# Linear attention's heads in staggered turns with finer steps, its gates' silu moved, weights cast further ahead in three jobs, and loads on GpSimd's queue

## The chip, the cores and the metric

The kernel runs on one core of a Trainium2 chip. A core has five engines with instruction streams of their own: TensorE (PE, with its weight loads as PEld), VectorE (DVE), ScalarE (ACT), GpSimd (POOL) and SyncE (SP). Each runs its stream in order; streams wait for each other by semaphores. Transfers between the device's memory and the core are issued by an engine onto its queue: SP and POOL do that here. The metric is the device time of one execution in microseconds, as the median of several runs.

## The reference

One layer of an encoder with 512 tokens and a width of 2048, in float32. The projection of the normalised input feeds two groups of heads, whose outputs are joined and projected; a gated feed-forward layer follows.

```python
h = rmsnorm(x) ; P = h @ W_in
# group A: 16 heads x 64, three dilated windows, merged
# group B: 4 heads of gated linear attention (dk 128, dv 256), both directions
G    = cumsum(log_a, within a chunk)
q_in = q * exp(G) ; k_in = k * exp(-G)
A    = (q_in @ k_in.T) * tril          # inside the chunk
S_t  = diag(a_t) S_{t-1} + k_t^T v_t   # across chunks
out_B = rmsnorm_per_head(o_fwd + o_bwd) * silu(gate)
x = x + concat(out_A, out_B) @ W_out
x = x + swiglu(rmsnorm(x)) ; rmsnorm at the end
```

What the change touches is group B: the four linear-attention heads (called heads 0 to 3 below), their output gates, and the weights of the projections beside which they run.

## The kernel before

**Jobs.** The large products are jobs, run one after the other by `run_job`: after the front part gqk0 and gv0 (queries, keys and values of the first two heads), gqk1 and gv1 (of the other two), gr0 and gr1 (the output gates, each four banks of results), then four jobs of the output projection, wo0 to wo3, then the feed-forward part. A job has 16 weight halves; for each half PE runs four banks of three matmuls (high by high, high by low, low by high part of the split numbers), 12 of 128x512. Kind A of job (gqk, gr) stands on lines L336 to L338, kind B (gv, wo) on L345 to L347.

**Weights.** `Stream` loads pieces of 512 KB on SP's queue (L209) into a few buffers and splits every half in two: ScalarE casts the high part (L237), VectorE subtracts it from the original (L218, the low part). At half i the split runs up to half i + AHEAD - 1 with AHEAD = 3. In the jobs called fine (gqk0 to gr1) the subtraction lags: it is issued at the next half's beginning. The load of a further piece waits in SP's stream until a buffer is free.

**Side work.** Beside the halves, `run_side` takes one step of the first `urgent` generator and one step of the `side` generator each time the credit reaches one; in a fine job the credit grows by a quarter of the job's rate after each bank (`RATES`, 2.5 for gqk and gv, 2.75 for gr), in wo by 1.0 after each half. The side generators are the low-rank forget gates, then the dilated attention (lines L536 to L700), then linear attention's heads.

**A head** (`gla`): softplus of the forget gates (L909 to L912), per direction a subtraction (L925), a scan along the tokens (L930), the chunk ends (L938 to L942), the centred sums (L945), exponentials (L943, L949, L950), the factors times queries and keys (L920), two products of PE with masks (L971, L977, L982, L991), the states between chunks (L1006 to L1025), the output products (L1053), a normalisation (L1061 to L1069), transposes (L1075) and a scaling (L1078). The heads run in pairs: `two(gla(0), gla(1))` takes one step of each in turn, started by the evacuation of gv0, and `two(gla(2), gla(3))` by that of gv1. A head's queries and keys, and a pair's values, are stored to memory by POOL (L825, L852) and come back by `load_gla` on SP's queue (L838, L842).

**The gates.** `evac_gr` multiplies the four banks by the normalisation's factors (L863) into four tiles of 128x512, applies silu at once (L868), and, for each head that is done, multiplies the head's output by it (L877) and splits the product into high and low part for the output projection (L408, L409).

Of the kernel before, what the change touches and what calls it, by code (L numbers as in the profile page):

```python
# [15 lines left out]
F32 = mybir.dt.float32  # L16
# [102 lines left out]
def layer(nc, tc, x, attn_norm_w, w_in, rel_table, gw_f, gb_f, gw_b, gb_b, gla_norm_w, w_out,  # L119
# [7 lines left out]
    with tc.manual_schedule(), \  # L127
# [48 lines left out]
        EXP_LN, SILU = "natural_log_exp_and_others", "silu_and_others"  # L176
        state = {"credit": 0.0, "set": None, "ahead": 0.0, "big": 0}

# [109 lines left out]
        class Job:  # L288
            fine = False
            drop = None  # L290
            between = None
# [15 lines left out]
        def run_job(j):  # L307
# [392 lines left out]
        def attention():  # L700
# [6 lines left out]
            for u in range(UNITS + 6):  # L707
                h = u // 4
                if u < UNITS:
                    if u % 8 == 2:  # L710
                        read_qk(h // 2 + 1)
                    if u % 8 == 5 and h // 2 + 1 < NH // 2:
                        urgent.append(load_qk(h // 2 + 1))
                    while h // 2 not in ready:
                        run_urgent()
                if "mix" in at:
                    pr = at.pop("mix")
                    mixh[pr] = split_of(mixf.pop(pr), big=pr > 4)
# [12 lines left out]
                if u % 2 == 0:  # L731
                    run(att_mix, (u - 6) // 2, UNITS // 2)
                run(att_norm, u - 1)
                if 33 <= u < 36:
                    load_v(1, ((0,), (1,), (2, 3))[u - 33])
                if u == UNITS - 3:
                    load_gla(0)
                    load_gla(1)
# [12 lines left out]

# [7 lines left out]
        gq, gk, gv = {}, {}, {}  # L759
        gate = {}  # L760
        gout = {}
# [66 lines left out]

        gla_there = []
        loaded = set()  # L830

        def load_gla(h):
            if h in loaded or h // 2 not in gla_there:
                return
            loaded.add(h)
            for d, i in ((gq, 0), (gk, 2)):
                d[h] = s2.get()
                sp.dma_start(out=d[h].t, in_=gqd[h // 2 * 4 + i + h % 2])  # L838
            if h % 2 == 0:
                gv[h // 2] = [s4.get(F32, [P, 2, 512]) for _ in range(2)]  # L840
                for i in range(2):
                    sp.dma_start(out=gv[h // 2][i].t.rearrange("p b c -> p (b c)"), in_=gvd[h + i])  # L842

        def evac_gv(pr):
            def f(banks):
                for t in range(4):
# [4 lines left out]
                    if t % 2:  # L851
                        pool.dma_start(out=gvd[2 * pr + t // 2], in_=v.t.rearrange("p b c -> p (b c)"))  # L852
                        put(v)
                gla_there.append(pr)
                side.append(two(gla(2 * pr), gla(2 * pr + 1)))
            return f

        def evac_gr(pr):
            def f(banks):
                ts = []  # L860
                for i in range(4):
                    t = s2.get()
                    dve.tensor_tensor(t.t, banks[i].t, rb[1].t, op=OP.mult)  # L863
                    put(banks[i])
                    ts.append(t)
                tables(SILU)
                for i in range(4):
                    act.activation(ts[i].t, ts[i].t, AF.Silu)  # L868
# [3 lines left out]
            return f  # L872

        def gla_out(i):
            if i in gate and i in gout:
                t, o = gate.pop(i), gout.pop(i)
                dve.tensor_tensor(o.t, o.t, t.t, op=OP.mult)  # L877
                put(t)
                mixf[8 + i] = o
                if not hT:  # L880
                    mixh[8 + i] = split_of(mixf.pop(8 + i), big=True)

# [6 lines left out]
        def gla(h):  # L889
# [14 lines left out]
            las = []  # L904
            tables(EXP_LN)
            for d in range(2):
                bcol = wcol[:, (B_F, B_B)[d] + h:(B_F, B_B)[d] + h + 1]
                l, m = s2.get(), s2.get()
# [6 lines left out]
                yield  # L915
            fs, qs, ks = [], [], []

# [3 lines left out]

            for d in range(2):
                c = fb[d]
                m, l = las[d]
                dve.tensor_tensor(m.t, m.t, l.t, op=OP.subtract)  # L925
                put(l)
                if d:
                    times(0)
                g = s2.get()
                dve.tensor_tensor_scan(g.t[:, c], G["res"][d].t[:, c], m.t[:, c], 0.0,  # L930
                                       op0=OP.mult, op1=OP.add)
                put(m)
                mid, end = ((63, 127), (64, 0))[d]
                f = sc[d]

                g3 = r3(g)
                if d == 0:
                    dve.tensor_tensor(f[:, 0:3], g3[:, 0:3, end], g3[:, 0:3, mid], op=OP.subtract)  # L938
                    dve.tensor_tensor(f[:, 0:3], f[:, 0:3], g3[:, 1:4, mid], op=OP.add)
                else:  # L940
                    dve.tensor_tensor(f[:, 0:3], g3[:, 1:4, end], g3[:, 1:4, mid], op=OP.subtract)
                    dve.tensor_tensor(f[:, 0:3], f[:, 0:3], g3[:, 0:3, mid], op=OP.add)  # L942
                act.activation(f[:, 0:3], f[:, 0:3], AF.Exp, scale=1.0 / TAU)  # L943
                gm = s2.get()
                dve.tensor_tensor(r3(gm), g3, g3[:, :, mid:mid + 1].to_broadcast([P, 4, P]), op=OP.subtract)  # L945
                put(g)
                yield
                q, k = s2.get(), s2.get()
                act.activation(q.t, gm.t, AF.Exp, scale=1.0 / TAU)  # L949
                act.activation(k.t, gm.t, AF.Exp, scale=-1.0 / TAU)  # L950
                put(gm)
                fs.append(f)
                qs.append(q)
                ks.append(k)
                yield
            times(1)
            yield
            put(gq.pop(h), gk.pop(h))
# [3 lines left out]
            T, kt = [], []  # L962
            as_, trs, ts = [], [], []
            for d in range(2):
                ts.append(s2.get())
                pool.memset(ts[d].t, 0.0)
            for d in range(2):
                a = ps.get()
                for b in range(4):
                    c = slice(b * P, (b + 1) * P)  # L970
                    mm(a.t[:, c], ks[d].t[:, c], qs[d].t[:, c], start=True, stop=True)  # L971
                as_.append(a)
            for d in range(2):
                tr = ps.get()
                for b in range(4):
                    c = slice(b * P, (b + 1) * P)
                    pe.transpose(tr.t[:, c], ks[d].t[:, c], idn)  # L977
                put(ks[d])
                trs.append(tr)
            for d in range(2):  # L980
                a, tr, t = as_[d], trs[d], ts[d]
                dve.copy_predicated(r3(t), masks[:, d:d + 1, :].to_broadcast([P, 4, P]),  # L982
                                    a.t.rearrange("p (b c) -> p b c", c=P))
                put(a)
                T.append(t)
                kk = s2.get()
# [5 lines left out]
            put(T[1])  # L992
            yield
            if h == 1:
                load_gla(2)
                load_gla(3)

# [68 lines left out]
            for i in range(2):  # L1066
                for b in (2 * i, 2 * i + 1):
                    c = slice((b % 2) * 256, (b % 2 + 1) * 256)
                    act.activation(on.t[:, b], os_[i].t[:, c], AF.Copy, scale=rs[:, b:b + 1])  # L1069
            put(*os_)  # L1070
            yield
            for i in range(2):
# [7 lines left out]
                gout[2 * h + i] = o  # L1080
            for i in range(2):
                gla_out(2 * h + i)
            yield
# [98 lines left out]
        n_front = len(jobs)  # L1182
        RATES = (2.5, 2.75)
        for pr in range(2):
# [11 lines left out]
        for j in jobs[n_front:]:  # L1196
            j.fine = True

        x1 = {}
# [914 lines left out]
```

## Time and profile before

| what | us |
|---|---|
| median of three runs | 2212.36 |
| lowest and highest run | 2211.18, 2214.01 |
| the profiled execution, its own time | 2214.81 |
| its span in the profile | 2213.0 |
| start of gr0's first matmul in it | 551.38 |

The profile has a page (busy time by engine, the span in slices, queues, the chain that ended last, the costliest groups) and views of the trace behind it: lists of waits, rows of one engine in order of time, and windows with each engine's busy time. A row in order of time reads: start, duration, engine, line, operation, output <- input, shape, and in brackets the idle time before it with what ended it. Rows of equal instructions in a run are folded (x8). Names in the profile are those of buffer classes: `a` holds tiles of 128x512, `b` tiles of 128x1024 or a pair of halves, `ps` the banks of results, `gqd` and `gvd` the stored queries, keys and values.

### The profile page before, as it was taken

The page shows a single profiled execution, that of the slowest core. Times are in us where ns is not written, and L with a number is a line of the kernel's source. Part 1 is how long each engine was busy: PE and PEld are TensorE (multiplying, and loading weights), DVE is VectorE, ACT ScalarE, POOL GpSimd, SP SyncE. Part 2 cuts the span into 40 slices and gives each one's busy share as a digit, 9 for nine tenths or more (in the row PEclk, how much of TensorE's full clock was granted, in tenths as well). Part 3 has the DMA queues.
Part 4 walks back from the last instruction along what each step waited for, and adds up shares of the span by engine and source line. Part 5 has one row for each costly group of instructions (what it writes and reads, how often), then busy time and mean ns, then how long its engine had stood idle before and what let it go on. Part 6 is the DMA issues. An engine that isn't in the chain of part 4 may idle for free.

```text
span 2213.0 us, 34591 instructions
## 1 busy us (share of the span) xinstructions
PE 2170.9 (98%) x12618; PEld 1908.3 (86%) x12618; DVE 1771.1 (80%) x3072; ACT 1200.8 (54%) x2197; POOL 333.1 (15%) x462
## 2 busy tenths in 40 slices
PE   9999999999889999999999999999999999999998
PEld 7888778888768888988888888888888899999987
DVE  5698757775575675898899989899899888988885
ACT  7454456776455243555555555555555565565562
POOL 0011221110000120011221111221121220011300
PEclk9999999999989999999999999999999999999999
DMA  5377774544225884367776767776777876576982
GB/s 189 123 189 173 186 222 130 177 140 130 90 66 170 287 298 149 100 167 188 174 194 176 183 179 184 187 183 185 177 183 183 254 186 200 177 187 155 280 312 76
DMA packets 257368, 397.81 MB, mean 180 GB/s; under 512 B 18925, under 2 KB 154269, under 8 KB 257198
## 3 DMA queue, kind: packets, MB, share of 16 engines
q1 hardware_dynamic: 203134, 276.69, 39.3%
q0 software_dynamic: 53744, 118.39, 24.1%
q8 instruction: 99, 1.62, 0.3%
q14 instruction: 71, 0.58, 0.1%
q10 hardware_dynamic: 320, 0.53, 0.1%
HBM read 285.37 MB, written 64.29 MB: 158 GB/s over the span
## 4 chain that ended last, share of the span: by engine, by line
PE 82%; issue 6%; DMA 5%; DVE 4%; ACT 2%; POOL 0%; DVEq 0%; ACTq 0%; SPq 0%; POOLq 0%
PE ps L1465 25%; PE ps L1451 13%; PE ps L346 6%; PE ps L345 6%; PE ps L347 6%; PE ps L1815 5%; PE ps L1816 5%; PE ps L1814 5%; DMA b<-a 4%; PE ps L338 2%; PE ps L336 2%; PE ps L337 2%; PE ps L650 1%; PE ps L1053 1%; DVE b L1374 1%
## 5 line engine op out<-in xcount | busy, mean ns | idle before, releaser
L1369 ACT CAST b<-b 128x768 fp32r<-128x768 f32 (+1 forms) x537 | 488.8, 945 | 349.9 <-DVE b L1374 162.3
L1374 DVE TENSOR_TENSOR b<-b,b 128x768 fp32r<-128x768 f32 (+1 forms) x537 | 563.8, 1084 | 35.1 <-ACT b L1369 24.2
L1465 PE MATMUL ps<-b,b 128*128 128x512 f32 x1552 | 451.0, 393 | 0.4 <-ACT b L1369 0.2
L1465 PE MATMUL ps<-a,b 128*128 128x512 f32 x1248 | 365.7, 394 | 4.2 <-DVE b L1485 4.2
L1465 PEld LDWEIGHTS ps<-b,b 128*128 128x128 f32 x1552 | 263.5, 188 | 30.7 <-ACT b L1369 0.7
L1451 PEld LDWEIGHTS ps<-b,b 128*128 128x128 f32 x1552 | 252.8, 190 | 36.1
L1451 PE MATMUL ps<-b,b 128*128 128x256 f32 x1552 | 275.4, 280 | 0.0
L1451 PEld LDWEIGHTS ps<-a,b 128*128 128x128 f32 x1248 | 208.0, 189 | 34.2 <-DVE b L1374 0.4
L1465 PEld LDWEIGHTS ps<-a,b 128*128 128x128 f32 x1248 | 207.2, 189 | 24.3 <-ACT a L1497 4.9
L1451 PE MATMUL ps<-a,b 128*128 128x256 f32 x1248 | 223.7, 280 | 0.0
L1356 DVE TENSOR_TENSOR b<-b 128x512 f32<-128x512 f32 x244 | 167.3, 686 | 19.7 <-DMA b<-in_w_down_dram 8.0
L1814 PE MATMUL ps<-b,b 128*128 128x256 f32 x624 | 176.6, 283 | 0.0
L1816 PE MATMUL ps<-b,b 128*128 128x256 f32 x624 | 176.6, 283 | 0.0
L1815 PE MATMUL ps<-b,b 128*128 128x256 f32 x624 | 176.6, 283 | 0.0
L345 PE MATMUL ps<-b,b 128*128 128x512 f32 x348 | 138.8, 399 | 2.0 <-ACT b L237 2.0
L346 PE MATMUL ps<-b,b 128*128 128x512 f32 x348 | 136.7, 393 | 0.9 <-DVE b L218 0.9
L347 PE MATMUL ps<-b,b 128*128 128x512 f32 x348 | 136.4, 392 | 0.0
L1815 PEld LDWEIGHTS ps<-b,b 128*128 128x128 f32 x624 | 119.8, 192 | 0.0
L1816 PEld LDWEIGHTS ps<-b,b 128*128 128x128 f32 x624 | 119.8, 192 | 0.0
L1814 PEld LDWEIGHTS ps<-b,b 128*128 128x128 f32 x624 | 119.8, 192 | 0.0
L218 DVE TENSOR_TENSOR b<-b,b 128x512 fp32r<-128x512 f32 x150 | 100.1, 684 | 21.9 <-ACT b L237 21.8
L1358 DVE TENSOR_TENSOR b<-b,b 128x256 f32<-128x256 f32 x244 | 103.9, 426 | 8.4
(293 smaller groups left out, 4354.8 us busy)
## 6 DMA issues: line engine op xcount, KB each, us to landing
b<-in_w_gate_dram SPq DMA_DIRECT2D x109, 512.0 KB, 4.1
b<-in_w_up_dram SPq DMA_DIRECT2D x88, 512.0 KB, 4.3
b<-in_w_down_dram SPq DMA_DIRECT2D x88, 512.0 KB, 8.0
b<-in_w_in_dram SPq DMA_DIRECT2D x78, 512.0 KB, 4.0
b<-a POOLq DMA_DIRECT2D x150, 256.0 KB, 4.5
b<-in_w_out_dram SPq DMA_DIRECT2D x32, 512.0 KB, 5.9
gd<-b POOLq DMA_DIRECT2D x22, 512.0 KB, 4.0
b<-gd SPq DMA_DIRECT2D x22, 512.0 KB, 7.8
```

Of the source, the lines that this page charges most:

```text
L345: mm(o, xh.t[:, c], wh.t[:, w], start=first and not on, stop=False, skip_group_check=on)
L346: mm(o, xh.t[:, c], wl.t[:, w], start=False, stop=False, skip_group_check=on)
L347: mm(o, xl.t[:, c], wh.t[:, w], start=False, stop=last, skip_group_check=on)
L1356: dve.tensor_tensor(s_[:, :, 0:2], r[:, :, 1:3], r[:, :, 0:1].to_broadcast(shape), op=OP.add)
L1358: dve.tensor_tensor(s_[:, :, 3], s_[:, :, 2], r[:, :, 3], op=OP.add)
L1369: act.copy(o, src)
L1374: dve.tensor_tensor(o, src, h, op=OP.subtract)
L1451: mm(o, wl, xh, start=False, stop=end, skip_group_check=True)
L1465: mm(o.rearrange("p (s t) -> p s t", s=2), wh, x_, start=first and p == 0, stop=False, skip_group_check=True)
L1814: mm(o, xh[:, t], wh, start=first and h == 0, stop=False, skip_group_check=True)
L1815: mm(o, xh[:, t], wl, start=False, stop=False, skip_group_check=True)
L1816: mm(o, xl[:, t], wh, start=False, stop=last, skip_group_check=True)
```

## The change

- **Turns.** `turns(heads, APART)` replaces `two`: one generator for all four heads, started at gv0's end. Up to two heads run in alternation; the next may start every 12 rounds, so that heads stand at different steps.
- **Finer steps.** The middle of a head is cut into `less`, `scan`, `centre`, `exps` and `times` per direction, with a yield after one or two of them; the masks' products are cut by direction.
- **Rate.** `RATES[1]` goes from 2.75 to 3.5 in gr0 and gr1.
- **Gates.** `evac_gr` only multiplies, into two tiles of 128x1024. A new urgent generator, `gates`, begins when head 3's normalisation is done: one silu on 128x1024 per tile (L880), then, one step later, for the two heads' halves of that tile the multiply (L884) and the split (L409 on ScalarE, L410 on VectorE), and in the same step the silu of the next tile. Head 3's scaling no longer triggers its gates.
- **Lead.** Jobs gv1, gr0 and gr1 cast up to half i + 4 at half i (`lead = 5`); the others keep 3.
- **Loads.** `load_gla` (queries and keys) and the new `load_gv` (values) issue on POOL's queue (L838, L843), each head's when it needs them.

Lines move by the inserted code: L218 and L237 stay, matmuls of kind A are L337 to L339, of kind B L346 to L348; in a head L912 becomes L919, L920 L965, L925 L928, L930 L934, L938 to L942 L946 and L947, L943 L958, L945 L949, L949 and L950 L956 and L957, L971 L997, L977 L1000, L982 L1003, L991 L1011, L1006 L1022, L1015 L1031, L1025 L1041, L1053 L1069, L1061 L1077, L1069 L1085, L1075 L1093, L1078 L1096. L408 becomes L409, L409 L410, L645 L646, L650 L651, L825 L829, L852 L853, L868 L880, L877 L884, and the feed-forward part's sums L1425 become L1444.

```diff
         class Job:
             fine = False
+            lead = AHEAD
...
-                st.split(j.first + i + (min(AHEAD, i + 1) if j.between else AHEAD) +
+                st.split(j.first + i + (min(AHEAD, i + 1) if j.between else j.lead) +
...
-        def two(a, b):
-            todo = deque((a, b))
-            while todo:
-                try:
-                    next(todo[0])
+        def turns(todo, apart):
+            now, n = deque(), 0
+            while todo or now:
+                if n % apart == 0 and todo:
+                    now.append(todo.popleft())
+                for _ in range(2):
+                    if _ < len(now):
+                        g = now[0]
+                        now.rotate(-1)
+                        if next(g, 0) == 0:
+                            now.remove(g)
+                            continue
                     yield
-                    todo.rotate(-1)
-                except StopIteration:
-                    todo.popleft()
+                n += 1
...
             for d, i in ((gq, 0), (gk, 2)):
                 d[h] = s2.get()
-                sp.dma_start(out=d[h].t, in_=gqd[h // 2 * 4 + i + h % 2])
-            if h % 2 == 0:
-                gv[h // 2] = [s4.get(F32, [P, 2, 512]) for _ in range(2)]
-                for i in range(2):
-                    sp.dma_start(out=gv[h // 2][i].t.rearrange("p b c -> p (b c)"), in_=gvd[h + i])
+                pool.dma_start(out=d[h].t, in_=gqd[h // 2 * 4 + i + h % 2])
+        def load_gv(pr):
+            gv[pr] = [s4.get(F32, [P, 2, 512]) for _ in range(2)]
+            for i in range(2):
+                pool.dma_start(out=gv[pr][i].t.rearrange("p b c -> p (b c)"), in_=gvd[2 * pr + i])
...
-                gla_there.append(pr)
-                side.append(two(gla(2 * pr), gla(2 * pr + 1)))
+                if pr == 0:
+                    side.append(turns(deque(gla(h) for h in range(NG)), APART))
...
         def evac_gr(pr):
             def f(banks):
-                ts = []
+                ts = [s4.get(F32, [P, 2, 512]) for _ in range(2)]
                 for i in range(4):
-                    t = s2.get()
-                    dve.tensor_tensor(t.t, banks[i].t, rb[1].t, op=OP.mult)
+                    dve.tensor_tensor(ts[i // 2].t[:, i % 2], banks[i].t, rb[1].t, op=OP.mult)
                     put(banks[i])
-                    ts.append(t)
+                raw_gate.extend(ts)
+                if side:
+                    return
+                urgent.append(gates())
+            return f
+        def gates():
+            yield
+            while raw_gate:
                 tables(SILU)
-                for i in range(4):
-                    act.activation(ts[i].t, ts[i].t, AF.Silu)
-                    gate[pr * 4 + i] = ts[i]
-                for i in range(4):
-                    gla_out(pr * 4 + i)
...
+                act.activation(t.t, t.t, AF.Silu)
+                yield
+                for i in range(2):
+                    o = gout.pop(n + i)
+                    dve.tensor_tensor(o.t, o.t, t.t[:, i], op=OP.mult)
+                    mixf[8 + n + i] = o
+                    if not hT:
+                        mixh[8 + n + i] = split_of(mixf.pop(8 + n + i), big=True)
...
+            less(0)
+            scan(0)
+            yield
+            centre(0)
+            less(1)
+            yield
+            exps(0)
+            scan(1)
+            yield
+            centre(1)
+            yield
+            times(0)
+            exps(1)
+            yield
             times(1)
+            if h % 2 == 0:
+                load_gv(h // 2)
             yield
...
+            if h == NG - 1:
+                urgent.append(gates())
...
-        RATES = (2.5, 2.75)
+        RATES = (2.5, 3.5)
+        APART = 12
...
+        for j in jobs[n_front + 3:]:
+            j.lead = 5
```

VectorE's rows at the beginning of gr0 (a and b are buffers, numbered by place and by use; L218 is a weight's low part, the others are steps of a head). Before, from one L218 to the one after the pair's scans:

```order
L218 TENSOR_TENSOR b17_447_5622<-b6_439_5513,b17_447_5622 128x512
L925 TENSOR_TENSOR a33_395_5599<-a33_395_5599,a3_394_5598 128x512
L930 SCALAR_TENSOR_TENSOR a1_402_5664<-a25_102_2649,a33_395_5599 128x512
L938 TENSOR_TENSOR small_76<-a1_402_5664 128x3
L939 TENSOR_TENSOR small_76<-small_76,a1_402_5664 128x3
L945 TENSOR_TENSOR a6_403_5669<-a1_402_5664 128x512
L925 TENSOR_TENSOR a35_397_5628<-a35_397_5628,a10_396_5627 128x512
L930 SCALAR_TENSOR_TENSOR a34_404_5675<-a25_102_2649,a35_397_5628 128x512
L938 TENSOR_TENSOR small2_77<-a34_404_5675 128x3
L939 TENSOR_TENSOR small2_77<-small2_77,a34_404_5675 128x3
L945 TENSOR_TENSOR a5_405_5680<-a34_404_5675 128x512
L218 TENSOR_TENSOR b18_448_5655<-b6_439_5513,b18_448_5655 128x512
```

Now, twelve rows of the same place:

```order
L218 TENSOR_TENSOR b28_446_5581<-b6_438_5446,b28_446_5581 128x512
L919 TENSOR_SCALAR a29_391_5625<-ps4_266_5575,wcol_74 128x512
L928 TENSOR_TENSOR a30_389_5593<-a30_389_5593,a10_388_5592 128x512
L934 SCALAR_TENSOR_TENSOR a35_392_5637<-a25_102_2649,a30_389_5593 128x512
L218 TENSOR_TENSOR b17_450_5616<-b26_441_5512,b17_450_5616 128x512
L946 TENSOR_TENSOR small_76<-a35_392_5637 128x3
L947 TENSOR_TENSOR small_76<-small_76,a35_392_5637 128x3
L949 TENSOR_TENSOR a2_395_5654<-a35_392_5637 128x512
L928 TENSOR_TENSOR a29_391_5625<-a29_391_5625,a33_390_5624 128x512
L218 TENSOR_TENSOR a16_394_5641<-b26_441_5512,a1_393_5640 128x512
L934 SCALAR_TENSOR_TENSOR a32_398_5673<-a7_103_2650,a29_391_5625 128x512
L946 TENSOR_TENSOR small_76<-a32_398_5673 128x3
```

Two heads' scans and sums stood together between two subtractions; now one direction of one head is worked on at a time, with a L218 after every three or four rows.

ScalarE's rows around wo0's beginning. Before, with the four silu of gr1's evacuation first (L237 casts weights, L408 the heads' outputs):

```order
L174 ACT_TABLE_LOAD
L868 ACTIVATE a10_496_6720<-a10_496_6720 128x512
L868 ACTIVATE a34_497_6722<-a34_497_6722 128x512
L868 ACTIVATE a17_498_6724<-a17_498_6724 128x512
L868 ACTIVATE a22_499_6726<-a22_499_6726 128x512
L237 CAST b15_500_6752<-b3_493_6643 128x512
L408 CAST b32_503_6771<-a30_440_6087 128x512
L237 CAST b21_504_6775<-b3_493_6643 128x512
L408 CAST b23_506_6794<-a23_441_6094 128x512
L237 CAST b22_507_6797<-b12_496_6689 128x512
L408 CAST b10_509_6817<-a2_442_6110 128x512
L237 CAST b14_510_6820<-b12_496_6689 128x512
```

Now, from the table's load that precedes the first silu (L880), with L409 for the heads' outputs:

```order
L174 ACT_TABLE_LOAD
L880 ACTIVATE b17_475_6152<-b17_475_6152 128x1024
L409 CAST b32_505_6775<-a19_429_5977 128x512
L409 CAST b7_506_6779<-a23_430_5984 128x512
L880 ACTIVATE b1_476_6153<-b1_476_6153 128x1024
L237 CAST b10_507_6783<-b28_495_6610 128x512
L409 CAST b16_509_6804<-a29_458_6268 128x512
L409 CAST b20_510_6808<-a16_459_6275 128x512
L880 ACTIVATE b3_500_6706<-b3_500_6706 128x1024
L237 CAST b24_511_6812<-b28_495_6610 128x512
L409 CAST b31_513_6832<-a17_487_6521 128x512
L409 CAST b9_514_6836<-a10_488_6528 128x512
```

Casts of weights and of outputs alternated one to one behind the silu; now two casts of outputs and a silu stand ahead of each weight cast, from wo0's fifth half (b10) on.

VectorE's rows at the same place of the changed kernel, where L884 is the multiply by the gate, L410 the output's low part, L218 the weight's low part and L1444 sums of the feed-forward part's weights:

```order
L884 TENSOR_TENSOR a19_429_5977<-a19_429_5977,b17_475_6152 128x512
L410 TENSOR_TENSOR b32_505_6775<-a19_429_5977,b32_505_6775 128x512
L884 TENSOR_TENSOR a23_430_5984<-a23_430_5984,b17_475_6152 128x512
L410 TENSOR_TENSOR b7_506_6779<-a23_430_5984,b7_506_6779 128x512
L218 TENSOR_TENSOR b10_507_6783<-b28_495_6610,b10_507_6783 128x512
L1444 TENSOR_TENSOR b23_503_6739<-b23_503_6739 128x2x128
L1444 TENSOR_TENSOR b6_504_6741<-b6_504_6741 128x2x128
L884 TENSOR_TENSOR a29_458_6268<-a29_458_6268,b1_476_6153 128x512
L410 TENSOR_TENSOR b16_509_6804<-a29_458_6268,b16_509_6804 128x512
L884 TENSOR_TENSOR a16_459_6275<-a16_459_6275,b1_476_6153 128x512
L410 TENSOR_TENSOR b20_510_6808<-a16_459_6275,b20_510_6808 128x512
L218 TENSOR_TENSOR b24_511_6812<-b28_495_6610,b24_511_6812 128x512
```

Each L410 needs the cast L409 of the product in the row above it, and each L218 the cast L237 behind the silu; before, a L218 stood between single L409 rows.

More of the change, by code (lines that the diff above doesn't have):

```diff
@@ L176, in layer @@
         EXP_LN, SILU = "natural_log_exp_and_others", "silu_and_others"
-        state = {"credit": 0.0, "set": None, "ahead": 0.0, "big": 0}
+        state = {"credit": 0.0, "set": None, "ahead": 0.0, "big": 0, "gates": 0}
         class Stream:
@@ L920, in times @@
                     dve.tensor_tensor(x_.t, x_.t, y.t, op=OP.mult)
[L922 to L955, printed above, removed]
+            less(0)
[12 more added lines that the diff above has]
+            yield
             times(1)
+            if h % 2 == 0:
+                load_gv(h // 2)
             yield
@@ L978, in gla @@
                 put(ks[d])
[L979 to L982, printed above, removed]
+                yield
+                dve.copy_predicated(r3(T[d]), masks[:, d:d + 1, :].to_broadcast([P, 4, P]),
                                     a.t.rearrange("p (b c) -> p b c", c=P))
                 put(a)
-                T.append(t)
                 kk = s2.get()
```

71 lines of the change are left out of this document (42 added, 29 removed).

## The prediction

> **What bounds the kernel now.** I read the page first, then the list of PE's waits, then PE and VectorE row by row where those waits lie.
>
> ```profile
> span 2213.0 us, 34591 instructions
> PE 2170.9 (98%) x12618; PEld 1908.3 (86%) x12618; DVE 1771.1 (80%) x3072; ACT 1200.8 (54%) x2197; POOL 333.1 (15%) x462
> ```
>
> TensorE is busy 98% of the span, so time can only be won where it stands still or runs at a lower clock. The change touches the jobs from gqk0 to wo0, and the instruction sequences agree again from the sixth half of wo0 on. The list of PE's waits from 540 to 720 us holds nearly all that can be won there (waited for; total, times, longest):
>
> ```profile
> PE ps L338 <- DVE b L218: 15.7, 6, 5.5
> PE ps L971 <- DVE a L920: 2.3, 1, 2.3
> PE ps L346 <- DVE b L218: 0.8, 1, 0.8
> ```
>
> That is 15.7 + 2.3 + 0.8 = 18.8 us: seven waits for the low part of a weight half (L218), one for a head's factors (L920). The windows (PE, PEld, DVE, ACT, POOL busy; granted clock) show where, and a second loss:
>
> ```profile
> 560.00:570.00 10.00, 5.21 (x22) 3.69 (x21) 9.76 (x20) 3.73 (x9) 1.07 (x2) 1.00 0.01 2
> 630.00:640.00 10.00, 6.02 (x14) 4.29 (x15) 9.79 (x18) 5.27 (x11) 0.00 (x0) 0.66 0.00 0
> 640.00:650.00 10.00, 4.53 (x16) 3.35 (x15) 9.76 (x19) 4.54 (x11) 2.10 (x4) 0.77 0.09 11
> 670.00:680.00 10.00, 10.00 (x47) 8.49 (x46) 1.83 (x4) 2.86 (x11) 0.00 (x0) 1.00 0.33 106
> ```
>
> VectorE is full (9.8 of 10) exactly where PE starves, and nearly idle (1.83) 30 us later: it is not short of time, its work comes in bunches, where two heads of a pair do the same steps together. The clock column falls to 0.66 and 0.77. PE's rows say how much that is:
>
> ```profile
> 564.94 0.50 PE L338 MATMUL ps<-b,b 128*128 128x512 f32 x1 [3.27 <-DVE b L218]
> 565.75 0.39 PE L338 MATMUL ps<-b,b 128*128 128x512 f32 x1
> ...
> 633.16 0.80 PE L338 MATMUL ps<-b,b 128*128 128x512 f32 x1 [3.40 <-DVE b L218]
> 633.75 0.63 PE L336 MATMUL ps<-b,b 128*128 128x512 f32 x1
> 634.18 0.63 PE L337 MATMUL ps<-b,b 128*128 128x512 f32 x1
> ...
> 640.04 0.39 PE L337 MATMUL ps<-b,b 128*128 128x512 f32 x1
> 640.27 0.40 PE L338 MATMUL ps<-b,b 128*128 128x512 f32 x1
> ...
> 647.95 0.79 PE L338 MATMUL ps<-b,b 128*128 128x512 f32 x1 [5.47 <-DVE b L218]
> ...
> 651.10 2.49 PE L971 MATMUL ps<-a,a 128*128 128x128 f32 x16
> 653.43 1.04 PE L977 MATMUL ps<-idn,a 128*128 128x128 f32 x8
> 654.23 0.48 PE L336 MATMUL ps<-b,b 128*128 128x512 f32 x1
> ...
> 655.68 1.95 PE L971 MATMUL ps<-a,a 128*128 128x128 f32 x16
> ```
>
> At full clock one matmul starts 0.23 us after another (640.04, 640.27), so a half of 12 takes 2.72. After the gaps of 3.40 and 5.47 us they start 0.43 apart (633.75, 634.18), after the gap of 3.27 they don't. About 12 matmuls lose 0.2 each after the first gap (2.4 us); after the second some 7, and the L971 group (2.49 against 1.95), lose 2.0. So **18.8 + 4.4 = 23.2 us** can go between 551 and 712 us.
>
> **What removes it.** Today half i+2 is cast at half i and its low part queued at i+1: one half, 2.7 us, before PE wants it. With lead 5 the cast is of half i+4, so three halves, 8.2 us, are left in gv1, gr0 and gr1. The longest wait, 5.47, is about the 5.4 gained. The bunches shrink too: before, VectorE does ten operations of two heads, two scans among them, between two L218 at gr0's start; after, three or four there, never with a second scan. I count all 23.2 as removed; L965 (old L920) of head 0 comes out 0.25 us ahead of PE when I lay its rows behind one another, so I charge 0.3 there (0 to 0.5), and 0.2 for head 2's products behind the multiply in gr1 (0 to 0.5).
>
> **The loads.** The list of SP's own waits has
>
> ```profile
> SPq L838 <- DVE a L920: 19.6, 2, 19.4
> ```
>
> so SP stands 19.4 us before a head's load, with the weight loads behind it, and yet every PE wait above is for VectorE, none for a transfer. Moving the twelve loads to POOL costs POOL 0.6 us each (the 2.34 below for four) and frees nothing that PE waits for: 0, or 0.5 if a load comes late behind a store.
>
> **A new wait in gv1.** The two extra leading casts (L237) are made at gv1's start. The second takes a buffer whose content POOL is just writing out, and stands ahead of the attention's scaling (L646, old L645) on ScalarE:
>
> ```profile
> 487.43 2.34 POOL L825 DMA_DIRECT2D gqd<-a  x4 [12.39 <-DVE a L820]
> gqd<-a POOLq DMA_DIRECT2D x4, 256.0 KB, 5.2
> 491.75 0.72 ACT L645 ACTIVATE a<-a,small 128x512 f32<-128x512 f32 x1
> 493.48 0.60 PE L650 MATMUL ps<-idn,a 128*128 128x128 f32 x4
> ```
>
> The store lands at 487.43 + 5.2 = 492.6; cast, cast and scaling (0.52 + 0.52 + 0.72) end at 494.4, while PE wants the scaled tile at 493.48: **1.0 us** (0 if the store lands early, 2 if late).
>
> **A new wait in gr1.** Durations for this and the next part (mean ns in the last figures before the idle time):
>
> ```profile
> L237 ACT CAST b<-b 128x512 fp32r<-128x512 f32 x42 | 25.1, 624 | 13.6 <-DVE b L1425 5.7 <-DVE b L409 4.0 <-DVE b L218 2.5
> L868 ACT ACTIVATE a<-a 128x512 f32<-128x512 f32 x8 | 4.7, 625 | 10.0 <-DVE a L863 9.9
> L1369 ACT CAST b<-b 128x1024 fp32r<-128x1024 f32 x265 | 279.0, 1053 | 67.6 <-DVE b L1374 49.2 <-DVE b L1358 15.1 <-PE ps L1816 1.1
> L930 DVE TENSOR_TENSOR_SCAN a<-a,a 128x512 f32<-128x512 f32 x8 | 9.8, 1221 | 0.1
> L218 DVE TENSOR_TENSOR b<-b,b 128x512 fp32r<-128x512 f32 x43 | 28.9, 684 | 0.3 <-ACT b L237 0.3
> L409 DVE TENSOR_TENSOR b<-a,b 128x512 fp32r<-128x512 f32 x10 | 6.9, 686 | 1.2 <-ACT b L408 1.2
> L877 DVE TENSOR_TENSOR a<-a,a 128x512 f32<-128x512 f32 x8 | 5.0, 686 | 0.1
> L1078 DVE TENSOR_SCALAR a<-ps,wcol 128x512 f32<-128x512 f32 x8 | 5.6, 747 | 10.1 <-PE ps L1075 10.1
> L1425 DVE TENSOR_TENSOR b<-b 128x256 f32<-128x256 f32 x31 | 12.4, 419 | 0.3
> L1069 ACT ACTIVATE b<-ps,small 128x256 f32<-128x256 f32 x16 | 6.2, 491 | 0.7 <-DVE small L385 0.7
> ```
>
> At gr1's start VectorE has, after the last multiply of gr0 (0.7), a scan (1.2), eight operations of 0.6 (three of them L218), seven small ones of some 0.17 with 0.3 for their returns from ScalarE, and then ScalarE's four L1085 (old L1069), 1.5 in a row: 9.7 us after gr0's end. PE wants their result for the transposes L1093 after 2.75 halves (7.5) and one direction of L997 and L1000 (half of 1.8 and of 0.8, from 655.68 and 653.43 above): 8.8. **1.0 us** (0 to 2).
>
> **The new wait in wo0.** This is the large one. Before, the silu, the multiply by the gate and the splits ran in a block at wo0's start, with its 0.8 us of wait. After, the urgent job `gates` does one step per half of wo0: multiply, cast, subtract, multiply, cast, subtract, and the silu of the next pair. Each hands over between VectorE and ScalarE, and the cast of the next weight half (L237) with its L218 is queued behind the step, since wo0 keeps the lead of 3. A hand-over costs next to nothing:
>
> ```profile
> 542.13 0.43 DVE L693 TENSOR_TENSOR a<-ps,a 64x256 f32<-64x256 f32 x1 [3.31 <-ACT a L684]
> 542.59 0.62 ACT L408 CAST b<-a 128x512 fp32r<-128x512 f32 x1 [0.49 <-DVE a L693]
> 543.24 0.69 DVE L409 TENSOR_TENSOR b<-a,b 128x512 fp32r<-128x512 f32 x1 [0.69 <-ACT b L408]
> ```
>
> (0.03 us each). The silu on 128x1024 is not in the trace; it lies between one of 128x512 (0.62) and two (1.25); I take 1.0, by the cast of that size issued back to back. One turn: multiply 0.72, cast 0.65, subtract 0.60, multiply 0.72, cast 0.52, silu 1.0, weight cast 0.65, L218 0.60, two L1444 (old L1425) 0.75: **6.2 us**, where PE eats a half in 2.72. The turn of the last pair has no silu (5.3).
>
> The first turn starts when head 3's last transposes are scaled, behind wo0's first half W: 2.7 + 0.5, two scalings 1.4 and two L1444 to W+5.3. Low parts then stand ready at W+10.9 for half 4, 17.1 for half 5, 23.3 for half 6 and 28.5 for half 7. PE, with 0.8 for the transposes, wants half 4 at 11.7 (in time), 5 at 14.5, 6 at 17.2, 7 at 19.9. The wait grows to 28.5 - 19.9 = **8.6 us**, in gaps of about 2.4, 3.5 and 2.7 us with the high parts 0.7 earlier, so that PE stands whole for about 2, 3 and 2. After half 7 the queue is empty and half 8's weights are early. With the silu at its ends the sum is 7.5 to 9.4; if half 4's cast passes the first step, 5; if other rows of this stretch fall between, 12.
>
> A rule bears on these gaps: "TensorE: Matmul & The Clock Gate" of the Trainium skill, section "Why this matters for your kernels", says to leave no idle gap over about 3 us between bursts, or the clock falls back to half. This trace agrees with the 3.4 us window of its Part 1: 3.27 kept the clock, 3.40 lost it. By the 3 us the gap before half 6 would just do it: 12 matmuls at 0.43 are 2.4 longer, of which half 7's own wait of 2.7 absorbs all, so the sum stays unless the slow stretch lasts into half 7 (up to 2.4 more).
>
> **Sum.** 23.2 - 0.3 - 0.2 - 1.0 - 1.0 - 8.6 = **12 us** gained. The profiled execution took 2214.81 (its span 2213.0 and 1.8 around it), so 2202.8 there. The three runs' median, 2212.36, is 2.45 below it; on that scale the forecast is **2200.4 us**.
>
> **Rivals.** (1) wo0's wait doesn't appear, since the steps are passed by the weight casts or fit into the front part of the half: gain 20.5, **2192**. For it: VectorE is only 1.83 of 10 busy at 670 to 680. Against it: the turn is a chain of hand-overs, not a load. 0.15. (2) The small new waits are all at their upper ends (2 + 2 + 0.5 + 0.5), wo0 gives back 12, or the clock falls there into half 7: gain 4.5 to 8, **2204 to 2208**. 0.12. (3) The change doesn't do what it says: heads still meet, the low parts still come late, and only the lead's first halves win: gain 0 to 4, **2208 to 2212**. Against it: in the new order three or four head operations stand between two L218 where ten stood. 0.06. (4) Slower: the chain of steps in wo0. Each microsecond more per turn costs 3 us by half 7, so the 20.7 left are eaten from a turn of 6.2 + (20.7 - 8.6)/3 = 10.2 us, and 0.2% is lost from 11.7, **2217** and over. It needs 0.8 us more in each of the seven hand-overs, where 0.03 is measured. 0.05.
>
> **Chances.** The forecast (gain 8 to 17, 2195 to 2204) has 0.62. Faster by over 0.2% (4.4 us, about what a measurement of this kernel can tell from no change) are the forecast, (1) and (2): 0.89; within it (3): 0.06; slower (4): 0.05. The range takes in the forecast and the nearer parts of (1) and (2): 2191 to 2207.
>
> **What would show it.** Right: no wait of PE for L218 between 551 and 682, clock 1.00 in all windows there, gr1 ending near 683 instead of 704; waits for L237 and L218 in wo0's halves 5 to 7 of 2 to 3.5 us with DVE and ACT alternating L884, L409, L410, L880. Wrong: waits for L218 left in gr0 or gr1 (the lead doesn't do), waits for transfers (POOL's queue), waits of over 2 us for L1085 or L965 (the finer steps come late), or none in wo0.

## The result, and the profile after

| | before | changed |
|---|---|---|
| median of four runs, us | 2212.97 | 2201.02 |
| lowest and highest | 2211.18, 2214.01 | 2197.47, 2201.28 |
| profiled execution, its span | 2214.81, 2213.0 | 2200.88, 2199.1 |

The ratio is 0.9943, 95% interval 0.9926 to 0.996: faster by 12 us, where 2200.4 was forecast. The list of PE's waits from 480 to 760 us (in total, times, longest) of the changed kernel:

```profile
PE ps L346 <- ACT b L237: 4.5, 3, 1.8
PE ps L651 <- ACT a L646: 2.3, 1, 2.3
PE ps L347 <- DVE b L218: 0.8, 3, 0.3
PE ps L619 <- DVE b L665: 0.5, 1, 0.5
```

No wait for L218 in gr0 or gr1 is left, none for the factors (L965); new ones are in gv1 (L646, and L665 behind it) and wo0 (L237, with L218 behind it). The windows of the stretches shown before, and of wo0:

```profile
560.00:570.00 10.00, 10.00 (x58) 8.72 (x57) 8.15 (x15) 4.26 (x10) 1.11 (x2) 1.00 0.69 238
630.00:640.00 10.00, 10.00 (x48) 8.35 (x46) 5.95 (x10) 7.59 (x16) 0.00 (x0) 1.00 0.14 48
640.00:650.00 10.00, 10.00 (x47) 8.45 (x46) 8.39 (x17) 5.23 (x18) 1.05 (x2) 1.00 0.30 86
700.00:710.00 10.00, 8.20 (x24) 5.48 (x24) 6.95 (x13) 3.48 (x6) 0.54 (x1) 0.83 0.55 188
```

PE is full at clock 1.00 where it stood at 5.21, 6.02 and 4.53; VectorE, 9.8 there before, has 6 to 8.4. Cut at the first matmuls of the stages, the two profiled executions differ so:

| stage | before, us | changed, us | difference | forecast |
|---|---|---|---|---|
| up to gv1 | 487.33 | 486.08 | -1.25 | 0 |
| gv1 | 64.05 | 67.02 | +2.97 | +1.0 |
| gr0 and gr1 | 154.67 | 130.63 | -24.04 | -21.7 |
| wo0, halves 0 to 7 | 22.90 | 31.32 | +8.42 | +8.6 |

Head 3's last transposes (0.8) moved from gr1 into wo0. The forecast for gr0 and gr1 is the 23.2 of the sum less the 0.8 of it that lie in wo0, less 1.5 for new waits, plus the 0.8 moved. The four measured rows add up to -13.9, the difference of the spans; the forecasts add up to -12.1. The first row is not of the change: that part runs the same instructions on PE, VectorE, ScalarE and GpSimd in every kernel here, and its end, gv1's first matmul, lies anywhere between 482.76 and 489.75 us in the fourteen traces. So a cause is read below from the stages behind it and not from a median alone.

### The profile page after: what moved, and what is told of

It reads as the page before. It is cut to its first block, busy times and chain, and to the rows that moved or that the text cites. A ratio compares the mean times of both kernels' runs of the same rounds, so it can differ in the third digit from the quotient of the medians.

```text
span 2199.1 us, 34574 instructions
## 1 busy us (share of the span) xinstructions
PE 2167.3 (99%) x12618; PEld 1905.0 (87%) x12618; DVE 1771.7 (81%) x3072; ACT 1195.8 (54%) x2190; POOL 339.2 (15%) x474
## 4 chain that ended last, share of the span: by engine, by line
PE 84%; issue 6%; DMA 4%; DVE 3%; ACT 1%; POOL 1%; DVEq 0%; SPq 0%; ACTq 0%; POOLq 0%
PE ps L1484 27%; PE ps L1470 13%; PE ps L347 5%; PE ps L348 5%; PE ps L346 5%; PE ps L1834 5%; PE ps L1835 5%; PE ps L1833 5%; DMA b<-a 2%; PE ps L337 2%; PE ps L339 2%; PE ps L338 2%; PE ps L651 1%; PE ps L1069 1%; PE ps L675 1%
## 5 line engine op out<-in xcount | busy, mean ns | idle before, releaser
L1484 PE MATMUL ps<-b,b 128*128 128x512 f32 x1552 | 451.7, 393 | 0.4 <-ACT b L1388 0.2
L346 PE MATMUL ps<-b,b 128*128 128x512 f32 x356 | 142.1, 399 | 8.0 <-ACT b L237 8.0
L347 PE MATMUL ps<-b,b 128*128 128x512 f32 x356 | 140.3, 394 | 1.9 <-DVE b L218 1.9
L348 PE MATMUL ps<-b,b 128*128 128x512 f32 x356 | 140.1, 393 | 0.0
L218 DVE TENSOR_TENSOR b<-b,b 128x512 fp32r<-128x512 f32 x146 | 97.8, 685 | 23.9 <-ACT b L237 23.8
```

Of the source, the lines that this page charges most:

```text
L346: mm(o, xh.t[:, c], wh.t[:, w], start=first and not on, stop=False, skip_group_check=on)
L347: mm(o, xh.t[:, c], wl.t[:, w], start=False, stop=False, skip_group_check=on)
L348: mm(o, xl.t[:, c], wh.t[:, w], start=False, stop=last, skip_group_check=on)
L1484: mm(o.rearrange("p (s t) -> p s t", s=2), wh, x_, start=first and p == 0, stop=False, skip_group_check=True)
```

## Experiments

Medians are of four to ten runs, each kernel's runs beside runs of the kernel before (medians 2213.5 to 2214.6). Ratios are to those; as those runs drift too (2207 to 2217), a ratio and a difference of two medians can disagree by some us.

### What gives the gain: the lead or the staggering

**Lead alone**, in the kernel before:

```diff
+            lead = AHEAD
-                st.split(j.first + i + (min(AHEAD, i + 1) if j.between else AHEAD) +
+                st.split(j.first + i + (min(AHEAD, i + 1) if j.between else j.lead) +
+        for j in jobs[n_front + 3:]:
+            j.lead = 5
```

> The kernel before with nothing but the lead of 5 in gv1, gr0 and gr1; heads in pairs, gates in a block, loads on SP. Theory (the lead gives 5.4 us more slack at each wait, but the pairs' bunches need more: in gr0 they add up to 6.0, in gr1 to 9.7 us): 5 to 9 us of waits stay, the wait of L920 at 575 us among them; gv1 gains its wait of some 2 us; wo0's block of gates costs 1 us as before: 2199 to 2205. Rival A (the lead alone suffices): no waits in gr0 and gr1 but L920's 2.3, 2194 to 2196. Rival B (the lead does nothing without the staggering): 2212.

2216.19, ratio 1.001 (1.0001 to 1.002). Neither the theory's 2199 to 2205 nor rival A; the time is nearest to rival B's, though the lead is not without effect. PE's waits in this kernel (L921 is the factors, old L920):

```profile
PE ps L972 <- DVE a L921: 19.5, 4, 7.3
PE ps L651 <- ACT a L646: 2.2, 1, 2.2
PE ps L619 <- DVE b L665: 0.5, 1, 0.5
```

The lead does what it is made for: all 15.7 us of waits for L218 are gone. But 19.5 us of waits for the factors stand in their place, before 2.3, and gr0 and gr1 take 155.55 us, before 154.67. The longest of these waits, on PE and on VectorE:

```profile
578.34 2.08 PE L972 MATMUL ps<-a,a 128*128 128x128 f32 x8 [7.32 <-DVE a L921]
573.06 1.28 DVE L921 TENSOR_TENSOR a<-a,a 128x512 f32<-128x512 f32 x2
574.26 1.22 DVE L931 TENSOR_TENSOR_SCAN a<-a,a 128x512 f32<-128x512 f32 x1
...
575.79 0.69 DVE L946 TENSOR_TENSOR a<-a 128x512 f32<-128x512 f32 x1
576.39 0.68 DVE L218 TENSOR_TENSOR b<-b,b 128x512 fp32r<-128x512 f32 x1
576.99 2.49 DVE L921 TENSOR_TENSOR a<-a,a 128x512 f32<-128x512 f32 x4
```

The bunch is as long as it was (from the scan to the four factors 5.2 us; the same rows of the kernel before, at 571.15, take 5.2); PE, no longer held at the weights, reaches the heads' products sooner and waits there for the end of the same bunch (7.3 us, to 578.34).

**All but the lead**: the changed kernel with

```diff
-            j.lead = 5
+            j.lead = 3
```

> The changed kernel with the lead of 3 in all jobs; turns, finer steps, gates and loads as changed. Theory (both parts are needed; staggered heads put at most some 3 us of VectorE work between two low parts, about the 2.7 us that a lead of 3 leaves): PE waits again for L218 in gr0 and gr1, in several waits under 1.5 us each, 2 to 6 us in all; the wait of 2.8 us in gv1 goes, wo0's 8.65 stay: 2200 to 2204. Rival A (the lead is what removes the waits): 15 us or more of L218 waits and half clock again, 2213 or over. Rival B (staggering alone removes them): no L218 wait at all, 2198.

2198.27, ratio 0.9923 (0.9908 to 0.9938): rival B. Its waits from 480 to 760 us are wo0's alone:

```profile
PE ps L346 <- ACT b L237: 5.3, 3, 2.6
PE ps L347 <- DVE b L218: 0.8, 3, 0.3
```

gr0 and gr1 take 130.61 us, in the changed kernel 130.63. With the heads staggered, a lead of 3 is enough; the lead of 5 only costs gv1's wait.

**Turns, with their rate, alone**: the kernel before with `turns` (12 rounds apart) in place of `two`, and

```diff
-        RATES = (2.5, 2.75)
+        RATES = (2.5, 3.5)
+        APART = 12
```

> The kernel before with turns (12 rounds apart) and the rate of 3.5 alone: coarse steps, lead of 3, gates in a block, loads on SP. Theory (the staggering is the cause of the gain, since it takes the bunches away): most of the 23.2 us go although nothing else is changed; 2 to 7 us of waits for L218 stay, where a scan and two factors stand between two low parts and where gr0's block of gates stands at gr1's start; no wait in gv1 and 1 us in wo0: 2192 to 2198. Rival (the finer steps are the cause): 12 us or more of waits for L218 and the factors, 2203 and over.

2198.32, ratio 0.9937 (0.9921 to 0.9954): the whole of the change's gain, from coarse steps and the old gates. The time is at the theory's upper end, the place is another: the waits for L218 in gr0 and gr1 are 0.2 us; one of 4.5 us is for L1075 (head 1's scaled output) at gr1's start. ScalarE there:

```profile
618.44 1.28 ACT L174 ACT_TABLE_LOAD   x1
619.74 2.20 ACT L874 ACTIVATE a<-a 128x512 f32<-128x512 f32 x4
621.84 0.61 ACT L237 CAST b<-b 128x512 fp32r<-128x512 f32 x1
622.46 1.28 ACT L949 ACT_TABLE_LOAD   x1
625.82 0.20 ACT L949 ACTIVATE small<-small 128x3 f32<-128x3 f32 x1 [2.07 <-DVE small L948]
626.03 1.28 ACT L174 ACT_TABLE_LOAD   x1
```

The silu block with its three table loads, and VectorE's multiplies beside it, stand ahead of the head's last steps. gr0 and gr1 take 140.6 us here, 134.0 with the finer steps and the silu still early (last run of the next part), 130.6 in the changed kernel: this is what the finer steps and the later silu take away, and the steps beside wo0 give back 8.4.

**Pairs with the finer steps**: the changed kernel at a lead of 3, with

```diff
-                if n % apart == 0 and todo:
-                    now.append(todo.popleft())
+                now = deque(todo.popleft() for _ in range(2))
```

and one step of each of the two until both are done.

> The changed kernel with the lead of 3 and with the heads in pairs again (two heads step by step, then the other two), all else as changed: finer steps, rate, gates, loads. Theory (staggering is the cause): the bunches are back, up to ten operations of two heads between two low parts, so 12 to 20 us of waits for L218 or the factors in gr0 and gr1, and wo0's 8.65 on top: 2210 to 2222. Rival (finer steps and rate are the cause): under 4 us of such waits, 2198 to 2202, as with the turns at lead 3 (2198.3).

2208.37, ratio 0.9983 (0.9974 to 0.9993):

```profile
PE ps L339 <- DVE b L218: 11.1, 5, 3.0
PE ps L993 <- DVE a L961: 0.7, 1, 0.7
PE ps L993 <- DVE a L999: 0.5, 1, 0.5
```

12.3 us of waits, as the theory has it; the time is lower than it said since wo0 lost nothing: in pairs the heads ended before gr1 did, gr0's gates were done beside gr1, and two turns were left for wo0. Against the lead-3 kernel above, which differs in the turns alone, staggering saves 10 us by the medians although it puts wo0's loss in; in gr0 and gr1 it saves 20.7 (151.35 to 130.61). The rate of 3.5 is in both, so it does not suffice without staggering; staggering at the old rate of 2.75 was not run.

### The loss in wo0

**The order inside a step** (both multiplies, both casts, both subtractions):

```diff
-                    o = gout.pop(n + i)
-                    dve.tensor_tensor(o.t, o.t, t.t[:, i], op=OP.mult)
-                    mixh[8 + n + i] = split_of(mixf.pop(8 + n + i), big=True)
+                for i in range(2):
+                    dve.tensor_tensor(os[i].t, os[i].t, t.t[:, i], op=OP.mult)
+                for i in range(2):
+                    act.copy(prs[i][0].t, os[i].t)
+                for i in range(2):
+                    dve.tensor_tensor(prs[i][1].t, os[i].t, prs[i][0].f, op=OP.subtract)
```

> The changed kernel with each gate step in another order: both multiplies, both casts, both subtractions, then the silu of the next pair. Same instructions, same step per half. Chain theory: VectorE no longer stands for each cast, the turn falls from 6.2 to about 4.9 us, low parts of half 5 come in time, halves 6 and 7 wait 2.0 and 1.0 us; the loss falls from 8.65 to about 3 us, 2195.5. Rival (load of the two engines, not the order): no change, 2201.

2195.52, ratio 0.9913 (0.9897 to 0.993); waits in wo0 1.3 and 0.5 us, and from one turn's L884 to the next 4.7 to 4.9 us instead of 6.2. **And a step's end behind each split:**

```diff
                         mixh[8 + n + i] = prs[i]
+                yield
```

> As the run with both multiplies first, and in addition a step's end between the split of one pair and the silu of the next, so that a weight cast of its own half comes between them, and a pair takes two halves. Chain theory: a turn of two halves is about 5.5 us on VectorE against 5.44 of PE, so no wait of PE for L237 or L218 in wo0; the whole 8.65 us come back, about 2192.4. Rival: gate work delays wo0 wherever it stands; the same instructions over eight halves still cost several us, 2196 to 2201.

2193.68, ratio 0.991 (0.9895 to 0.9924), and no wait in wo0. Its windows there:

```profile
690.00:700.00 10.00, 10.00 (x46) 8.26 (x45) 9.71 (x19) 5.92 (x10) 0.54 (x1) 1.00 0.51 169
700.00:710.00 10.00, 10.00 (x46) 8.29 (x45) 9.66 (x20) 5.63 (x10) 1.07 (x2) 1.00 0.83 287
```

PE is full with VectorE at 9.7 of 10, in the changed kernel PE lost 1.8 of 10 with VectorE at 6.95. So it was the chain, not the load.

**The lead of 5 in wo0 too** (`if c == 0: j.lead = 5`):

> The changed kernel with the first output job, wo0, also cast up to half i+4 at half i. Chain theory (the 8.65 us that wo0 gives back come from weight casts queued behind a turn of about 6.2 us per half of gate work): two more weight halves go ahead of the chain, so halves 5 to 7 come in time and the wait moves to halves 8 and 9, where it reaches about 4.5 us; gain about 4 us over the changed kernel, 2197. Rival (the loss is gate work as such, or slow transfers of the weights in wo0): no change, 2201, with the same waits at halves 5 to 7.

2196.52, ratio 0.9926 (0.991 to 0.9943). Two waits of 1.0 and 1.7 us, at 706 and 711 us instead of three from 700 on: a lead moves the chain's wait back, and what it doesn't reach is saved.

**Silu at once** (the silu back in `evac_gr`, the other steps left beside wo0):

> The changed kernel with the silu right behind gr0's and gr1's multiplies, as before; the multiply and the splits stay in the steps beside wo0. Theory (the later silu pays little, since what costs is the chain in wo0): each turn loses the silu only (6.2 to about 5.2 us), so wo0's loss falls from 8.65 to about 5.5; at gr1's start two silu and two table loads (4.7 us of ScalarE) stand ahead of head 1's and head 2's steps and PE waits some 2 to 4 us for L1085 or the factors there: 2199 to 2203. Rival (the silu's place was a main part of the gain): waits of 6 us or more at gr1's start, 2205 and over.

2201.42, ratio 0.9958 (0.9943 to 0.9972), as in the changed kernel: 2.0 us of wait for the factors at gr1's start, 4.3 in wo0 instead of 5.3. The later silu makes gr0 and gr1 3.4 us shorter and wo0 2.6 longer, so its place alone pays next to nothing.

### gv1, the queue, and the best version

**The lead of 5 in gr0 and gr1 only** (`jobs[n_front + 4:]`):

> The changed kernel with the lead of 5 in gr0 and gr1 only, not in gv1. Theory (the wait of 2.3 us for L646 at gv1's second half, and 0.5 behind it, comes from the third leading cast, whose buffer is being written out by POOL): that wait goes, 2.3 to 2.8 us less, 2198.5, if the three leading casts at gr0's start make no new wait (they stand beside the first head's steps: up to 1 us). Rival (the wait comes from the attention itself, or from the loads on POOL's queue): the wait stays, 2201. Rival 2 (gr0's start needs gv1's lead): new waits for L218 in gr0's first halves of 2 us or more.

2199.4, ratio 0.9934 (0.9919 to 0.9948). The waits for L646 and L665 are gone, and gr0's start has 0.8 us: the theory, with a gain in the median (1.6 us) that the runs' spread doesn't resolve. In the traces gv1 becomes 3.4 us shorter, gr0 and gr1 1.35 longer.

**Loads back on SP** (`sp.dma_start` in `load_gla` and `load_gv`):

> The changed kernel with the heads' loads of queries, keys and values back on SP's queue. Theory (no PE wait in this stretch is for a transfer, so the queue does not matter): 2200 to 2202, the same PE waits as in the changed kernel. Rival (SP stands up to 19 us before such a load with the weight loads behind it, and a lead of 5 needs the weights earlier): PE waits for L237 in gr0 or gr1 whose casts wait for a transfer, 3 us or more, 2204 and over.

2201.37, ratio 0.9935 (0.9918 to 0.9952): the waits for L646, L237 and L218 are as in the changed kernel, only that for L665 (0.5) is not there, and none is for a transfer. The queue makes no difference that these runs show.

**Best**: order and step's end as above, and gv1's lead late (`AHEAD if i < j.late else j.lead`, with 6 for gv1):

> The kernel with both multiplies first and the silu in a step of its own, and in addition gv1's lead of 5 only from its seventh half on. Theory: wo0 stays without waits, and gv1's wait of 2.3 us for L646 goes since no cast takes the buffer that is being written out; gr0 keeps its three halves of reserve, so no wait appears there: 2.4 to 2.8 us less than that kernel's 2193.7, 2191. Rival (two more casts and low parts in one half of gv1 hold up the attention there): a wait of 1 us or more at gv1's seventh or eighth half, 2192 to 2194.

2188.89, ratio 0.9884 (0.9867 to 0.9901). **The same with the lead of 3 everywhere:**

> The kernel with both multiplies first and the silu in a step of its own, with the lead of 3 everywhere. Theory (the lead does nothing once the heads are staggered): no wait for L218 in gr0 and gr1, none in gv1, none in wo0: as the kernel with gv1's late lead, 2187 to 2191. Rival (the lead still buys reserve there): waits of 2 us or more in gr0 or gr1, 2191 to 2194.

2189.47, ratio 0.991 (0.9894 to 0.9926; one of four runs was at 2195.88). In both profiles the list of PE's waits from 480 to 760 us is empty. By the medians they take 12 us off the changed kernel, by the ratios 13 and 7. In the traces the two agree within 0.2 us in gv1, in gr0 and gr1, and in wo0, so the lead gives nothing here.

## Why the prediction came out

**Bounds: right, a little short.** Of the 18.8 us of waits and 4.4 of half clock, 0.8 lie in wo0 and 22.4 in gr0 and gr1. These became 23.2 us shorter without the transposes that moved, with 0.4 lost in a new way, so some 1.3 more was there. A restart costs more than its listed wait: that of 3.27 us starts 3.42 us after its matmul was due (561.52), and the matmul behind it comes after 0.34 instead of 0.23, 0.26 in all. gr1's end, 704 in the signs, is 706.05 in that trace.

**"What removes it": the number right, the cause wrong.** The prediction gave the gain first to the lead ("three halves, 8.2 us, are left") and the spreading second. The runs show the reverse: lead alone no gain, staggering (with its rate) alone 14 us by the ratio, 15 by the medians. The failed thought is that a wait is removed when the work waited for is queued earlier. VectorE was behind with all its work; a lead lets the weights pass and the factors come late.

**The closeness is partly luck.** 2200.4 was forecast and 2201.02 measured, but gv1 lost 2.0 us more than forecast and gr0 and gr1 gained 2.3 more, which nearly cancel.

**gv1: right mechanism, size 2.8 instead of 1.0 (0.9 by the sum's own figures, 494.4 less 493.48).** ScalarE's rows:

```profile
492.91 0.62 ACT L237 CAST a<-b 128x512 fp32r<-128x512 f32 x1 [4.66 <-DMA gqd<-a]
493.43 0.61 ACT L409 CAST b<-a 128x512 fp32r<-128x512 f32 x1
493.95 0.72 ACT L646 ACTIVATE a<-a,small 128x512 f32<-128x512 f32 x1
```

The scaling ends at 494.7, where 494.4 was worked out. But PE was there 1.25 us earlier than in the execution before, and the end of the store did not move with it: it was issued 1.4 us earlier (486.03) and took 6.8 us instead of 5.2. The next step, L665, was late by 0.5, which wasn't counted. So the step that was mis-sized is the store's time to landing, and the sum lies outside the 0 to 2 allowed for it.

**gr1's L1093: about 0.4 us instead of 1.0.** L1085 ended 9.4 us after gr0's last matmul (9.7 in the sum). PE came to the transposes after 8.7 (8.8) and took them one by one as L1085's four parts ended (1.25 us for the eight instead of 0.8), which the list doesn't show as a wait.

**wo0: right to 0.2 us.** The turns, from L884 to L884 (VectorE at 689.21, 695.37, 701.59, 707.68), are 6.16, 6.22 and 6.09 us, where 6.2 was worked out from the kernel before. One turn on VectorE:

```profile
694.09 0.69 DVE L218 TENSOR_TENSOR b<-b,b 128x512 fp32r<-128x512 f32 x1 [0.78 <-ACT b L237]
694.70 0.75 DVE L1444 TENSOR_TENSOR b<-b 128x256 f32<-128x256 f32 x2
695.37 0.68 DVE L884 TENSOR_TENSOR a<-a,b 128x512 f32<-128x512 f32 x1
696.74 0.69 DVE L410 TENSOR_TENSOR b<-a,b 128x512 fp32r<-128x512 f32 x1 [0.69 <-ACT b L409]
697.35 0.69 DVE L884 TENSOR_TENSOR a<-a,b 128x512 f32<-128x512 f32 x1
698.72 0.69 DVE L410 TENSOR_TENSOR b<-a,b 128x512 fp32r<-128x512 f32 x1 [0.69 <-ACT b L409]
700.18 0.69 DVE L218 TENSOR_TENSOR b<-b,b 128x512 fp32r<-128x512 f32 x1 [0.77 <-ACT b L237]
```

The brackets are the chain: in the turn from 695.37 to 701.59 VectorE stands 2.2 of 6.2 us for casts. The silu on 128x1024 took 1.05 us (1.0 in the sum), and the low parts were ready 11.1, 17.1, 23.4 and 28.6 us after wo0's start (10.9, 17.1, 23.3 and 28.5). The listed waits of the halves (2.0, 1.3 and 1.9 us, 5.3 in all) are less than the 8.4 lost and than the 2 to 3.5 of the signs; of the rest some 1.6 is half clock in half 5, and the remainder the restarts behind the waits.

**The rivals.** Rival (1), wo0 without a wait, was not so, and not far: the other order and a step's end together give it (the step's end alone was not run). Rival (3), that heads still meet and low parts come late, did not come; but the lead, the queue and the silu's place, three parts of the change, pay nothing by themselves here. Of rival (2), the clock did fall in wo0, but in half 5, where it cost nothing. Rival (4), a longer turn, did not come. Without wo0's 8.6 the sum gives 20.7, where rival (1) has 20.5.

## What to carry to other kernels

When an engine's work comes in bunches, queueing one consumer's share earlier can move the wait to the next consumer, as it did here; spreading the bunch removed it. Find out by doing the lead alone. A step that goes back and forth between two engines holds up whatever is queued behind it by its length, not by its load: do all of the first engine's part, then all of the second's, and end the step where the next urgent thing should pass.

## What was not expected of the hardware

The clock doesn't fall by the length of a gap alone. In the kernel before, 3.27 us of idle kept it and 3.40 lost it. But gv1's gap, 2.2 to 2.4 us in seven traces, kept it in four (the four transposes behind it took 0.66 us) and lost it in three (the runs with wo0's lead, with the step's end and with SP's loads; 1.11 to 1.12 us). In wo0 of the changed kernel it fell behind two short ones:

```profile
700.21 0.49 PE L346 MATMUL ps<-b,b 128*128 128x512 f32 x1 [1.79 <-ACT b L237]
700.93 0.54 PE L347 MATMUL ps<-b,b 128*128 128x512 f32 x1 [0.23 <-DVE b L218]
701.27 0.63 PE L348 MATMUL ps<-b,b 128*128 128x512 f32 x1
701.70 0.63 PE L346 MATMUL ps<-b,b 128*128 128x512 f32 x1
...
704.91 0.40 PE L348 MATMUL ps<-b,b 128*128 128x512 f32 x1
```

The clock records of the traces show what decides. In every trace the granted clock changes only at the bounds of stretches of 3.41 us that follow one another without a break. Windows cut at these bounds (length, PE's busy time first; the clock is the third number from the end), four of the kernel before and two of the changed kernel:

```profile
560.08:563.49 3.41, 1.60 (x7) 0.96 (x6) 3.27 (x7) 0.20 (x1) 0.00 (x0) 1.00 0.02 5
563.49:566.90 3.41, 1.96 (x9) 1.62 (x10) 3.38 (x7) 2.81 (x6) 0.54 (x1) 1.00 0.00 0
628.34:631.76 3.42, 1.41 (x7) 0.83 (x5) 3.29 (x6) 3.41 (x6) 0.00 (x0) 1.00 0.35 129
631.76:635.17 3.41, 2.01 (x5) 1.63 (x6) 3.33 (x6) 1.56 (x2) 0.00 (x0) 0.50 0.00 0
697.84:701.25 3.41, 1.38 (x5) 0.63 (x4) 1.92 (x5) 2.08 (x3) 0.00 (x0) 1.00 0.53 154
701.25:704.66 3.41, 3.41 (x9) 2.63 (x8) 2.32 (x4) 0.99 (x2) 0.00 (x0) 0.50 0.48 154
```

The gap of 3.27 us is split between two stretches, and in each PE is still busy for 1.60 us or more; that of 3.40, and the two short ones in wo0, leave 1.41 and 1.38 us, and the next stretch runs at half. So 3.27 and 3.40 are not two sides of a limit on the gap. From 480 to 760 us in the fourteen traces, all 15 stretches at full clock in which PE was busy for 0.43 or less of the time were followed by one at half; of the seven at 0.44 to 0.51 two were, and none of those above.

"TensorE: Matmul & The Clock Gate" of the Trainium skill has a free-running window (Part 1: The HAM clock gate); that the same gap falls to either side from run to run agrees with it, and so does the length of the stretches, but gaps well under one window lost the clock here. The half clock cost nothing in wo0, since half 6 waited for its weights anyway.
